# Two heads on one diagonal in the RWKV recurrence of a hybrid decoder step

## The chip, the cores and the metric

The kernel runs on one core of one Trainium2 chip. The metric is the device time of one execution in microseconds (us). A core has a matrix engine (PE, with PEld for its weight loads), three engines for elementwise work (DVE, ACT, POOL) and SP, which here issues every DMA. Each engine takes its instructions in the order in which they were written into its queue before the run.

## The reference

One layer of a decoder trunk on two groups that share the weights: one fresh sequence of 512 tokens, and 8 samples with 8 new tokens each and a past. An RMS norm and an input projection feed two mixers side by side: an RWKV-7 recurrence with 8 heads of 64 channels, and an attention branch with compressed, selected and windowed keys (NSA). Both are gated, merged, projected and added to the residual, and a gated FFN follows. The recurrence is

```
S = S * w_t + (S a_t) b_t^T + v_t k_t^T        per head, S is 64 x 64
y_t = S r_t
```

for the 512 prompt tokens from a zero state, and for each sample's 8 tokens from the state given for it. All is f32.

## The kernel before

The 576 tokens are the free axis; channels lie on the 128 partitions. Weights and activations are split in a high and a low part, and each product of them is three matmuls; all of these are on line 359 (`mm3`). The input projection is 41 column tiles of 16 steps (two column cuts, 8 contraction blocks), and a step is three matmuls. They are generators in a queue called `tiles`, and `pull(n)` writes n steps of them into the program at the place where it is called. So the projection is the filler between the serial steps of the recurrence: `FILL` gives the tiles that are written ahead of the chain of each head pair, `PULL` the steps behind each half step of that chain.

The recurrence works on four pairs of heads, i = 0 to 3. For each pair `rw_operands` builds, for 8 chunks of 64 tokens and one ninth chunk that holds the 64 sample tokens, the operands and the strictly triangular 64 x 64 blocks of pairs of tokens (18 blocks: 9 chunks, 2 heads). The inverse of identity minus block is made in two parts. `rw_inverse` sends the 16 x 16 diagonal blocks through DRAM (`d1`) into 36 partitions of the tile `im`, solves them there on DVE in 15 steps, and sends the results back through DRAM (`d2`) into `dt` (the tile's name in a trace is invt), `b1` (named b), `wt` (in the tile yb) and the diagonal of the blocks. Then `rw_merge_inverse` joins 16 to 32 (lines 661, 668, 671) and 32 to 64 (lines 680, 686) on PE, with copies out of PSUM on ACT and DVE between the rounds. The blocks of both heads lie on partitions 64 to 127 of the state block (`gu`, the same bytes as `gb`), side by side on the free axis, and the 18 blocks go as two groups of nine. `rw_transposed_reads` turns the read operands (line 696) into `at`, which lies in the upper partitions of the tiles im and iw for even pairs, of bk0 and bk1 for odd ones. `rw_fold_inverse` multiplies them by the inverse, a matmul per chunk and head (line 704, 64 rows deep, 64 columns moving); then POOL clears gb's upper half (line 708), since the chain's second matmul reads all 128 rows of it.

`rw_chain` walks the 8 chunks in order (lines 803 and 812 on PE, with DVE between). `rw_samples` does the ninth chunk: it loads the samples' states of one head after the other and transposes them (line 716), reads them (line 733), scales them on POOL, transposes them back (line 743), adds the outer products (line 763) and stores them.

An f32 matmul appears as two MATMUL instructions in the trace, a transpose as one. `PS(tag)` takes the next PSUM bank of a small ring (two banks per pair's parity, tags c0 and c1), and a bank is written again when its reader is done. `slots.t(.., tag)` gives an SBUF slot by its tag. Instructions get their place on each engine from the order in which the code is written, from regions marked high priority (fold, merge and chain steps), and from a scheduler that plans with its own cost figures before the run; semaphores then keep the data right.

## Time and profile before

| what | us |
|---|---|
| median of 3 runs | 1191.52 (1177.23 to 1199.91) |
| the profiled execution's own time | 1183.65 |
| its span, first to last instruction | 1181.8 |
| PE busy in the span | 1128.9 |
| DVE, ACT, POOL busy | 729.4, 523.9, 244.5 |
| mean granted PE clock | 0.971 of full |

The program runs in stages that can be told by the instructions: the norm, the first projections and the operands of pairs 0 and 1 to about 150 us; the joins, chains and samples of the four pairs with projections between them from about 150 to 515; attention to about 650; gate merge, output projection and FFN to the end. The joins of 16 x 16 blocks begin at 154.0, 196.1, 348.5 and 410.3 us. The page gives busy times, which overlap between engines. A matmul's duration holds its whole way through the array, so matmuls that follow each other closely overlap in time; the room that each takes is read from how many follow each other in a stretch. PEclk is the PE clock that was granted, 1.00 being full.

### The profile page before, as it was taken

Reading aid. Unit: us, or ns where it says so; the run is one execution under the profiler, and the core shown is the slowest. Engines: PE = TensorE matmul, PEld = TensorE weight load, DVE = VectorE, ACT = ScalarE, POOL = GpSimd, SP = SyncE. Lnnn points to the kernel's source line nnn. Section 1 sums busy time; section 2 is a strip of 40 time slices with the busy share of each in tenths; the row PEclk is TensorE's granted clock in tenths of the full one; section 3 lists DMA queues with packets and bytes.
Section 4 is the critical chain, followed back from the end, with each engine's and each line's share of the span. In section 5 each row is a group of like instructions: output and inputs, shape, how many; then the busy total and the mean of one; then the engine's idle time right before and its main releaser. Section 6 shows DMA issues by size and latency. Waiting matters only on the chain.

```text
span 1181.8 us, 23148 instructions
## 1 busy us (share of the span) xinstructions
PE 1128.9 (96%) x9117; PEld 1067.7 (90%) x9117; DVE 729.4 (62%) x1461; ACT 523.9 (44%) x1096; POOL 244.5 (21%) x313
## 2 busy tenths in 40 slices
PE   6999899999999999889999999999999999999995
...
GB/s 183 75 59 97 77 88 94 57 59 69 77 145 83 87 133 90 138 31 83 112 104 53 165 152 89 109 37 133 102 70 90 72 142 73 56 89 72 90 72 81
DMA packets 194792, 108.95 MB, mean 92 GB/s; under 512 B 49780, under 2 KB 187970, under 8 KB 194682
## 3 DMA queue, kind: packets, MB, share of 16 engines
...
## 4 chain that ended last, share of the span: by engine, by line
PE 80%; DVE 8%; ACT 4%; DMA 4%; issue 2%; SPq 2%; POOL 0%; POOLq 0%; ACTq 0%; DVEq 0%
PE pd L359 46%; PE pu L359 10%; PE acc L1216 2%; PE ps L704 2%; PE ps L581 2%; SPq L152 1%; PE pT L1201 1%; PE ps L1037 1%; PE pS L1186 1%; DMA wraw<-in_w_in 1%; PE sm L396 1%; DVE invt L155 1%; PE pS L1188 1%; PE pq L733 1%; PE ps L696 1%
## 5 line engine op out<-in xcount | busy, mean ns | idle before, releaser
L359 PE MATMUL pd<-hh,whi 128*128 128x256 f32 (+1 forms) x656 | 203.7, 311 | 8.8 <-ACT pe L407 4.3
L359 PE MATMUL pd<-hh,wlo 128*128 128x256 f32 (+1 forms) x656 | 202.8, 309 | 2.7 <-DVE wlo L155 1.6
L359 PE MATMUL pd<-hl,whi 128*128 128x256 f32 (+1 forms) x656 | 201.5, 307 | 0.0
L359 PE MATMUL pd<-act,hi 128*128 128x288 f32 (+2 forms) x704 | 141.8, 296 | 0.0
L359 PEld LDWEIGHTS pd<-hh,whi 128*128 128x128 f32 x656 | 128.5, 196 | 11.9 <-ACT pe L407 6.3
L359 PEld LDWEIGHTS pd<-hh,wlo 128*128 128x128 f32 x656 | 128.5, 196 | 5.1 <-DVE wlo L155 2.0
L359 PEld LDWEIGHTS pd<-hl,whi 128*128 128x128 f32 x656 | 128.7, 196 | 1.4
L359 PEld LDWEIGHTS pd<-act,hi 128*128 128x128 f32 x704 | 112.6, 188 | 0.1
L155 DVE TENSOR_TENSOR wlo<-wraw,whi 128x1024 fp32r<-128x1024 f32 x60 | 81.0, 1351 | 43.8 <-ACT whi L337 40.0
L359 PE MATMUL pd<-act,lo 128*128 128x288 f32 (+2 forms) x352 | 103.8, 296 | 0.0
L359 PE MATMUL pd<-h2l,hi 128*128 128x288 f32 x352 | 103.6, 295 | 0.0
L359 PE MATMUL pd<-h2h,hi 128*128 128x288 f32 x352 | 103.1, 295 | 0.0
L359 PE MATMUL pd<-h2h,lo 128*128 128x288 f32 x352 | 103.1, 294 | 0.0
L337 ACT CAST hi<-wraw 128x1024 fp32r<-128x1024 f32 (+1 forms) x46 | 46.5, 1012 | 118.8 <-PE pd L359 62.5
L337 ACT CAST whi<-wraw 128x1024 fp32r<-128x1024 f32 x59 | 61.8, 1047 | 83.2 <-PE pd L359 52.7
L155 POOL TENSOR_TENSOR sg<-sg,ut 128x576 f32<-128x576 f32 x11 | 18.1, 1646 | 340.6 <-DVE ut L155 325.5
L155 DVE TENSOR_TENSOR x<-x,pd 128x288 f32<-128x288 f32 (+1 forms) x64 | 28.8, 451 | 65.4 <-PE pd L359 65.4
L155 DVE TENSOR_TENSOR lo<-wraw,hi 128x1024 fp32r<-128x1024 f32 (+1 forms) x46 | 57.0, 1240 | 19.0 <-ACT hi L337 18.8
L359 PEld LDWEIGHTS pd<-h2l,hi 128*128 128x128 f32 x352 | 66.1, 188 | 0.0
L359 PEld LDWEIGHTS pd<-act,lo 128*128 128x128 f32 x352 | 66.0, 188 | 0.0
L359 PEld LDWEIGHTS pd<-h2h,lo 128*128 128x128 f32 x352 | 66.0, 188 | 0.0
L359 PEld LDWEIGHTS pd<-h2h,hi 128*128 128x128 f32 x352 | 65.9, 188 | 0.0
...
## 6 DMA issues: line engine op xcount, KB each, us to landing
...
```

The lines of the kernel that those rows point to most:

```text
L152: (eng or nc.sync).dma_start(out, in_)
L155: return e.tensor_tensor(out, a, b, op)
L337: e[0](hi[:, 0:n], raw[:, 0:n])
L359: i_ = MM(pt[:, 0:w_], lhsT=w, rhs=x[:, c], start=first and k == 0 and j == 0, stop=last and k == n - 1 and j == 2, **kw)
L396: MM(pt[:, 0:HALF], lhsT=l, rhs=r[:, half(a)], start=i == 0, stop=i == len(terms) - 1)
L581: MM(pt[:, c * 128:(c + 1) * 128], lhsT=bk[0:64, c0 + c], rhs=ag[:, c0 + c], start=True, stop=True)
L696: TR(pt[0:64, c * 128:c * 128 + 128], S["ag"][h][:, c0 + c, 0:64], ident)
L704: MM(pw[:, x * 64:x * 64 + 64], lhsT=S["at"][h][:, c], rhs=S["gb"][64:128, c, h], start=True, stop=True)
L733: MM(pq4[0:64, h, :, b], lhsT=s0s[h][0:64, b * 64:b * 64 + 64], rhs=rv[:, :, b], start=True, stop=True)
L1037: MM(po, lhsT=w[:, sl_], rhs=z[:, l, :, hf:hf + 162], start=hf == 0 and l == 0 and j == 0, stop=hf == 1 and l == 7 and j == 2)
L1186: MM(pS[:, 0:nk], lhsT=qs[:, qt * 128:qt * 128 + 128], rhs=kh[:, 0:nk], start=True, stop=False, skip_group_check=True)
L1216: MM(po[:, c0:hf * 256 + 256], lhsT=lv, rhs=ptx[m][:, kk * 256 + q0:kk * 256 + 256], start=name == "slc" and hf == 0 and kt == 0 and j == ...
```

## The change

The two heads of a pair are put on one block diagonal. The pair blocks go to a new tile `nb` (128 rows, nine 128 x 128 squares), head 0 in rows and columns 0 to 63 and head 1 in 64 to 127; the rest of it is cleared once at the start on POOL. `at` becomes a tile of its own, with head 0's reads in rows 0 to 63 and head 1's in rows 64 to 127. Four such tiles are new (nb0, nb1, at0, at1); im and iw shrink from 1152 to 512 columns. The upper half of gb is cleared once at the start and no longer for each pair.

- Join: one group of nine chunks on four 32-row strips at a time, in place of two groups on two strips. The count of matmuls is the same; the copies on ACT go from ten to nine per pair, each group of a round from two PSUM banks to one.
- Fold: one matmul per chunk for both heads, 128 rows deep and 128 columns moving.
- Inverse: the same bytes through d1 and d2, in 8 and 14 DMAs per pair in place of 4 and 7.
- Samples: states of both heads stacked on the rows; 8 transposes in place of 16, 8 reads in place of 16 (with a reads tile `rv` that is zero across heads), one POOL scaling in place of two, 4 transposes back in place of 8, one addition on DVE in place of two. The loads are four DMAs in place of two.
- The keys of the attention branch move to the slots bk0 and bk1, its values to at0 and at1. `FILL` and `PULL` get other numbers, with the same sums.

```
-FILL = (12, 0, 6, 2)
-PULL = (3, 5, 3, 2)
+FILL = (10, 2, 6, 2)
+PULL = (4, 4, 3, 2)
...
+        nbs.extend(wide(x, x).rearrange("p (c x) -> p c x", x=128) for x in ("nb0", "nb1"))
+        ats.extend(wide(x, x).rearrange("p (c x) -> p c x", x=128) for x in ("at0", "at1"))
+        for t_ in nbs:
+            G.memset(t_, 0.0)
+        for t_ in state:
+            G.memset(t_[64:128, 4 * NTOK:8 * NTOK], 0.0)
...
+        S["nb"], S["at"] = nbs[i % 2], ats[i % 2]
...
-        for (rows, x) in ((slice(64, 128), 0), (slice(0, 64), 64)):
-            tt(V, gb[rows], pv_[0:64, :, x:x + 64], bc(mk[0:64, None, x:x + 64], [64, n, 64]), ALU.mult)
+        q = slice(h * 64, h * 64 + 64)
+        tt(V, nb[q, :, q], pv_[0:64, :, 0:64], bc(mk[0:64, None, 0:64], [64, n, 64]), ALU.mult)
+        tt(V, gb[0:64], pv_[0:64, :, 64:128], bc(mk[0:64, None, 64:128], [64, n, 64]), ALU.mult)
         tt(V, ag[64:128], pv_[64:128], bc(mk[64:128, None, :], [64, n, 128]), ALU.mult)
...
+        units = [(slice(h * 9, h * 9 + 9), k, h * 64 + k * 32) for h in range(2) for k in range(2)]
+        for u, k, o in units:
             for b in range(2):
-                o = k * 32 + b * 16
-                dma(d1[k, :, b].rearrange("u s t -> s u t"), gu[64 + o:80 + o, :, o:o + 16])
+                q = slice(o + b * 16, o + b * 16 + 16)
+                dma(d1[k, u, b].rearrange("u s t -> s u t"), nb[q, :, q])
...
+        for u, k, o in units:
+            G.tensor_copy(S["b1"][o:o + 16, :, 0:16], bc(ident[o:o + 16, None, o:o + 16], [16, 9, 16]))
+            dma(S["dt"][o:o + 16], d2[1, k, u, 0].rearrange("u s t -> s u t"))
+        for u, k, o in units:
+            dma(S["b1"][o + 16:o + 32, :, 16:32], d2[0, k, u, 1].rearrange("u s t -> s u t"))
+            if k == 0:
+                dma(S["wt"][o + 16:o + 32, :, 16:32], d2[1, 0, u, 1].rearrange("u s t -> s u t"))
+        for u, k, o in units:
+            q = slice(o + 16, o + 32)
+            dma(nb[q, :, q], d2[0, k, u, 1].rearrange("u s t -> s u t"))
 
     def rw_merge_inverse(S):
 
...
+        nb, dt, b1, wt, ct = (S[x] for x in ("nb", "dt", "b1", "wt", "ct"))
+        quarters, halves = (0, 32, 64, 96), (0, 64)
+        for o in quarters:
+            G.tensor_copy(nb[o:o + 16, :, o:o + 16], bc(ident[o:o + 16, None, o:o + 16], [16, 9, 16]))
+        pz = PS(ct)
+        for u in range(9):
+            for o in quarters:
+                MM(pz[o:o + 32, u * 16:u * 16 + 16], lhsT=nb[o:o + 16, u, o:o + 32], rhs=dt[o:o + 16, u], start=True, stop=True)
+        zt = slots.t(512, f"zt{S['i']}", f"zt{S['par']}")
+        A.copy(zt[:, 0:144], pz[:, 0:144])
+        pw = PS(ct)
+        for u in range(9):
+            z = zt[:, u * 16:u * 16 + 16]
+            for o in quarters:
+                MM(pw[o:o + 16, u * 32:u * 32 + 32], lhsT=z[o:o + 32], rhs=b1[o:o + 32, u], start=True, stop=True)
+            for o in halves:
+                MM(pw[o:o + 32, 288 + u * 16:304 + u * 16], lhsT=b1[o:o + 32, u], rhs=z[o:o + 32], start=True, stop=True)
+        for o in halves:
+            V.tensor_copy(wt[o:o + 32, :, 0:16], pw[o:o + 32, 288:432].rearrange("p (u t) -> p u t", t=16))
+        for o in quarters:
+            A.copy(nb[o:o + 16, :, o:o + 32], pw[o:o + 16, 0:288].rearrange("p (u t) -> p u t", t=32))
+        pz = PS(ct)
+        for u in range(9):
+            for o in halves:
+                MM(pz[o + 32:o + 64, u * 32:u * 32 + 32], lhsT=nb[o:o + 32, u, o + 32:o + 64], rhs=wt[o:o + 32, u],
                    start=True, stop=True)
+        zt = slots.t(512, f"zt{S['i']}", f"zt{S['par']}")
+        for o in halves:
+            A.copy(zt[o + 32:o + 64, 0:288], pz[o + 32:o + 64, 0:288])
+        pw = PS(ct)
+        for u in range(9):
+            for o in halves:
+                q = slice(o + 32, o + 64)
+                MM(pw[o:o + 32, u * 32:u * 32 + 32], lhsT=zt[q, u * 32:u * 32 + 32], rhs=nb[q, u, q], start=True, stop=True)
+        for o in halves:
+            A.copy(nb[o:o + 32, :, o + 32:o + 64], pw[o:o + 32, 0:288].rearrange("p (u t) -> p u t", t=32))
 
     def rw_transposed_reads(S):
-        for h in range(2):
-            for c0 in (0, 4, 8):
-                m = min(4, 9 - c0)
+        for c0 in (0, 4, 8):
+            m = min(4, 9 - c0)
+            for h in range(2):
                 pt = PS(S["ct"])
                 for c in range(m):
                     TR(pt[0:64, c * 128:c * 128 + 128], S["ag"][h][:, c0 + c, 0:64], ident)
-                A.copy(S["at"][h][:, c0:c0 + m], pt[0:64, 0:m * 128].rearrange("p (c x) -> p c x", x=128))
+                A.copy(S["at"][h * 64:h * 64 + 64, c0:c0 + m], pt[0:64, 0:m * 128].rearrange("p (c x) -> p c x", x=128))
 
     def rw_fold_inverse(S):
 
-        for cs in ([(c, 0) for c in range(8)], [(c, 1) for c in range(8)], [(8, h) for h in range(2)]):
+        for c0 in (0, 4, 8):
+            m = min(4, 9 - c0)
             pw = PS(S["ct"])
-            for x, (c, h) in enumerate(cs):
-                MM(pw[:, x * 64:x * 64 + 64], lhsT=S["at"][h][:, c], rhs=S["gb"][64:128, c, h], start=True, stop=True)
-            n, (c, h) = len(cs), cs[0]
-            A.copy(S["ag"][h][:, 0:8, 0:64] if n == 8 else S["agh"][:, 8, :, 0:64],
-                   pw[:, 0:n * 64].rearrange("p (c s) -> p c s", s=64))
-        G.memset(S["gb"][64:128], 0.0)
-
-    def rw_state(S, i, h):
-
-        s0 = slots.t(512, "s0n", f"zt{S['par']}")
-        dma(s0[0:64].rearrange("p (b j) -> p b j", b=8), I["state_rwkv"][0][:, 2 * i + h].rearrange("b i j -> i b j"))
+            for c in range(m):
+                MM(pw[:, c * 128:c * 128 + 128], lhsT=S["at"][:, c0 + c], rhs=S["nb"][:, c0 + c], start=True, stop=True)
+            A.copy(S["agh"][:, c0:c0 + m, :, 0:64],
+                   pw[:, 0:m * 128].rearrange("p (c h x) -> p c h x", h=2, x=64))
+
+    def rw_state(S, i):
+
         pt = PS(S["ct"])
-        for b in range(8):
-            TR(pt[0:64, b * 64:b * 64 + 64], s0[0:64, b * 64:b * 64 + 64], ident[0:64, 0:64])
-        s0t = slots.t(512, "s0t", f"s0{h}")
-        A.copy(s0t[0:64], pt[0:64])
+        for x in range(2):
+            s0 = slots.t(512, "s0n", f"zt{S['par']}")
+            s4 = s0[0:64].rearrange("p (b h j) -> p b h j", b=4, h=2)
+            for h in range(2):
+                dma(s4[:, :, h], I["state_rwkv"][0][4 * x:4 * x + 4, 2 * i + h].rearrange("b i j -> i b j"))
+            for b in range(4):
+                TR(pt[:, (4 * x + b) * 64:(4 * x + b) * 64 + 64], s0[0:64, b * 128:b * 128 + 128], ident[0:64, 0:64])
+        s0t = slots.t(512, "s0t", "s00")
+        A.copy(s0t, pt)
         return s0t
 
...
-        s0s = [rw_state(S, i, h) for h in range(2)]
+        s0t = rw_state(S, i)
+
+        rv = slots.t(512, "rv", "s01")[:, 0:256]
+        G.memset(rv, 0.0)
+        for h in range(2):
+            A.copy(rv[h * 64:h * 64 + 64].rearrange("p (b h x t) -> p h x b t", b=8, h=2, x=2)[:, h],
+                   ag[h][0:64, 8].rearrange("p (x b t) -> p x b t", x=2, b=8))
         pq = PS(ct, "pq")
-        pq4 = pq[:, 0:256].rearrange("p (h x b t) -> p h x b t", h=2, x=2, b=8)
-        for h in range(2):
-            rv = ag[h][0:64, 8].rearrange("p (x b t) -> p x b t", x=2, b=8)
-            for b in range(8):
-                MM(pq4[0:64, h, :, b], lhsT=s0s[h][0:64, b * 64:b * 64 + 64], rhs=rv[:, :, b], start=True, stop=True)
+        for b in range(8):
+            MM(pq[0:64, b * 32:b * 32 + 32], lhsT=s0t[:, b * 64:b * 64 + 64], rhs=rv[:, b * 32:b * 32 + 32], start=True, stop=True)
         sq = slots.t(512, "sq", f"zt{par}")
-        A.copy(sq[0:64, 0:256], pq[0:64, 0:256])
-
-        sos = []
-        for h in range(2):
-            s3 = s0s[h][0:64].rearrange("p (b i) -> p b i", b=8)
-            tt(G, s3, s3, bc(lam[0:64, h, 8:16, None], [64, 8, 64]), ALU.mult)
-            pt = PS(ct)
-            for x in range(4):
-                TR(pt[:, x * 64:x * 64 + 64], s0s[h][0:64, x * 128:x * 128 + 128], ident[0:64, 0:64])
-            so_ = slots.t(512, "so", f"s0{h}")
-            A.copy(so_[:, 0:256], pt[:, 0:256])
-            sos.append(so_)
+        A.copy(sq[0:64, 0:256].rearrange("p (y b t) -> p b y t", y=4, b=8), pq[0:64, 0:256].rearrange("p (b y t) -> p b y t", b=8, y=4))
+
+        s3 = s0t.rearrange("p (b i) -> p b i", b=8)
+        tt(G, s3, s3, bc(S["lams"][:, :, None], [128, 8, 64]), ALU.mult)
+        pt = PS(ct)
+        for x in range(4):
+            TR(pt[:, x * 128:x * 128 + 128], s0t[:, x * 128:x * 128 + 128], ident)
+        so_ = slots.t(512, "so", "s01")
+        A.copy(so_, pt)
...
+        pn = PS(ct)
         for h in range(2):
             ux = slots.t(512, "ux", f"zt{par}")
             tt(V, ux.rearrange("p (b i) -> p b i", b=8), bc(sv[:, 8, h][:, None, :], [128, 8, 64]),
                bc(khb[:, 8:16, None], [128, 8, 64]), ALU.mult)
-            pn = PS(ct)
             for x in range(4):
-                MM(pn[:, x * 64:x * 64 + 64], lhsT=ux[:, x * 128:x * 128 + 128], rhs=bt[:, 8, h], start=True, stop=True)
-            so_ = sos[h]
-            tt(V, so_[:, 0:256], so_[:, 0:256], pn[:, 0:256], ALU.add)
+                MM(pn[:, x * 128 + h * 64:x * 128 + h * 64 + 64], lhsT=ux[:, x * 128:x * 128 + 128], rhs=bt[:, 8, h],
+                   start=True, stop=True)
+        tt(V, so_, so_, pn, ALU.add)
+        o4 = so_.rearrange("p (x h j) -> p h x j", x=4, h=2)
+        for h in range(2):
             for b in range(2):
-                dma(O["s_rwkv"][0].rearrange("(x b) h i j -> b h i x j", b=2)[b, 2 * i + h],
-                    so_[b * 64:b * 64 + 64, 0:256].rearrange("p (x j) -> p x j", x=4))
+                dma(O["s_rwkv"][0].rearrange("(x b) h i j -> b h i x j", b=2)[b, 2 * i + h], o4[b * 64:b * 64 + 64, h])
...
-            t_ = wide(("im", "iw")[bi], "kst", dt=F32R)
+            t_ = wide(f"bk{bi}", "kst", dt=F32R)
...
-            vt = wide(f"bk{bi}", "vtok")
+            vt = wide(f"at{bi}", "vtok")```

Three places in the engines' order follow. In each row stand the source line, the operation and out<-in by the program's names with buffer numbers, and the shape. Lines 672 to 758 of the changed kernel are lines 661 to 743 of the kernel before: 689 and 698 join 32 to 64 (680 and 686 before), 717 folds (704 before).

PE, the second half of pair 0's join, before: 680 and 686 are the two rounds for the two groups of nine, 592 is a product of pair 1's operands, 359 is projection.

```order
L359 MATMUL pd_2042<-hh_98,whi_2038 128x256
L359 MATMUL pd_2042<-hl_99,whi_2038 128x256
L680 MATMUL ps_1562<-yb_941,state_316 32x32 x6
L686 MATMUL ps_1551<-state_316,zt_237_1549 32x32 x9
L680 MATMUL ps_1562<-yb_941,state_316 32x32 x3
L592 MATMUL ps_1332<-state_317,bk_85_320 128x128
L592 MATMUL ps_1332<-state_317,bk_86_321 128x128
L359 MATMUL pd_2042<-hh_98,wlo_2039 128x256
```

The same place now, with 599 and 604 (587 and 592 before) and 708 (696 before) from pair 1.

```order
L359 MATMUL pd_2069<-hl_101,whi_2065 128x256
L689 MATMUL ps_1579<-yb_957,nb_87_322 32x32
L359 MATMUL pd_2069<-hh_100,wlo_2066 128x256
L689 MATMUL ps_1579<-yb_957,nb_87_322 32x32 x17
L599 MATMUL ps_1348<-ident_63,bk_86_321 128x64 x8
L604 MATMUL ps_1358<-state_317,bk_85_320 128x128
L604 MATMUL ps_1358<-state_317,bk_86_321 128x128
L708 MATMUL ps_1463<-ident_63,state_317 64x128 x4
```

Before, the last round of the first group stood among the third round of the second group. Now all eighteen of a round stand together, and other work stands between the rounds.

PE, the fold of pair 0, before: state_316 holds the blocks, im_318 and iw_319 the transposed reads of head 0 and 1.

```order
L704 MATMUL ps_1585<-state_316,im_318 128x64 x3
L704 MATMUL ps_1595<-state_316,iw_319 128x64 x8
L600 MATMUL ps_1342<-ident_63,bk_85_320 128x64
L600 MATMUL ps_1342<-ident_63,bk_86_321 128x64
L696 MATMUL ps_1424<-ident_63,state_317 64x128 x4
L359 MATMUL pd_2070<-hh_98,wlo_2039 128x320
```

The fold of pair 0 now.

```order
L359 MATMUL pd_2132<-hh_92,whi_2128 128x256
L359 MATMUL pd_2132<-hl_93,whi_2128 128x256
L717 MATMUL ps_1622<-nb_87_322,at_89_324 128x128 x4
L717 MATMUL ps_1628<-nb_87_322,at_89_324 128x128 x4
L359 MATMUL pd_2132<-hh_92,wlo_2129 128x256
```

Half as many matmuls, each with 128 moving columns, and they stand in one block in the projection.

SP, the way of pair 0's solved blocks back from DRAM, before: d2p is the DRAM tile, b, invt, yb and state are where the blocks go, nsp and wraw belong to the projections.

```order
L152 DMA d2p_158_897<-iw_319 36x512
L152 DMA d2p_158_897<-im_318 36x512
L152 DMA nsp<-nsp_1969 128x320
L152 DMA b_160_940<-d2p_158_897 16x18x16
L152 DMA invt_906<-d2p_158_897 16x18x16 x2
L152 DMA b_160_940<-d2p_158_897 16x18x16
L152 DMA yb_941<-d2p_158_897 16x18x16
L152 DMA state_316<-d2p_158_897 16x18x16 x2
```

The same place now.

```order
L152 DMA d2p_162_909<-iw_319 36x512
L152 DMA nsp<-nsp_1996 128x320
L152 DMA wraw_2188<-in_w_in 128x8x64
L152 DMA d2p_162_909<-im_318 36x512
L152 DMA b_164_956<-d2p_162_909 16x9x16 x4
L152 DMA invt_922<-d2p_162_909 16x9x16 x4
L152 DMA yb_957<-d2p_162_909 16x9x16 x2
L152 DMA nb_87_322<-d2p_162_909 16x9x16 x4
```

Fourteen DMAs of half the size stand where seven stood, and the last invt load, which the join's first round reads, is now the eighth of them and not the third.

81 lines of the change are left out of this document (19 added, 62 removed).

## The prediction

> **What bounds the kernel now.** I read the page first, then the busy times by stage, then what PE waited for, then the groups of matmuls that the change touches, and the chain of waits where these stand. From the page, the span, PE's busy time and the chain by engine:
>
> ```profile
> span 1181.8 us, 23148 instructions
> PE 1128.9 (96%) x9117; PEld 1067.7 (90%) x9117; DVE 729.4 (62%) x1461; ACT 523.9 (44%) x1096; POOL 244.5 (21%) x313
> PE 80%; DVE 8%; ACT 4%; DMA 4%; issue 2%; SPq 2%; POOL 0%; POOLq 0%; ACTq 0%; DVEq 0%
> ```
>
> PE is busy for 96% of the span and is 80% of the chain, so the end moves with the work on PE, less what its waits take back. The stages, one row each (length, then PE, PEld, DVE, ACT and POOL busy, granted clock, DMA share and rate):
>
> ```profile
> 85.00:180.00 95.00, 89.03 (x853) 83.15 (x853) 54.25 (x115) 41.18 (x80) 24.98 (x39) 0.96 0.34 82
> 180.00:220.00 40.00, 40.00 (x507) 38.38 (x507) 18.08 (x53) 14.47 (x33) 2.15 (x6) 1.00 0.35 93
> 220.00:300.00 80.00, 80.00 (x609) 75.66 (x609) 53.05 (x105) 39.29 (x80) 24.20 (x24) 0.98 0.22 57
> 300.00:345.00 45.00, 42.50 (x321) 39.02 (x320) 32.86 (x73) 22.37 (x43) 14.98 (x20) 0.94 0.39 99
> 345.00:382.00 37.00, 37.00 (x446) 33.69 (x445) 17.13 (x30) 13.35 (x27) 11.16 (x9) 0.82 0.43 124
> 382.00:445.00 63.00, 60.70 (x631) 56.69 (x631) 40.46 (x97) 25.36 (x59) 15.18 (x17) 0.93 0.40 103
> 445.00:520.00 75.00, 70.68 (x521) 62.39 (x522) 47.92 (x130) 39.16 (x115) 29.15 (x45) 0.91 0.35 95
> ```
>
> These 435 us hold all that the change touches. PE stands idle in them for 435 - 419.9 = 15 us only, but its clock is below full, most of all (0.82) in the stretch that holds join and fold of pair 2. The granted clock lost 0.04 x 95 + 0.02 x 80 + 0.06 x 45 + 0.18 x 37 + 0.07 x 63 + 0.09 x 75 = 26 us of clock there. What PE waited for between 85 or 90 and 520 us (us in total, times, longest):
>
> ```profile
> PE pd L359 <- ACT nsp L887: 3.3, 1, 3.3
> PE ps L828 <- DVE so L155: 2.1, 1, 2.1
> PE ps L680 <- ACT gate L1345: 1.7, 1, 1.7
> ```
>
> These are the longest, and only the last is at a join. So the recurrence's serial steps are covered by projections, and a matmul that goes away there shortens the stage by about its own room.
>
> **The change part by part.** The groups on PE from 85 to 520 us that the change touches, and three of other shapes (581, 587, 696) that give prices; the first number behind the bar is the time in which one of the group was on PE, in us:
>
> ```profile
> L581 PE MATMUL ps<-state,bk 64*128 64x128 f32 x128 | 20.2, 297 | 0.0
> L696 PE MATMUL ps<-ident,state 128*64 128x128 f32 x72 | 13.2, 294 | 0.0
> L704 PE MATMUL ps<-state,bk 64*128 64x64 f32 x72 | 10.1, 284 | 0.0
> L671 PE MATMUL ps<-b,zt 32*16 32x32 f32 x288 | 9.9, 189 | 0.0
> L733 PE MATMUL pq<-state,s0t 64*64 64x16 f32 x128 | 9.7, 208 | 0.0
> L661 PE MATMUL ps<-invt,state 16*32 16x16 f32 x288 | 7.7, 179 | 0.0
> L680 PE MATMUL ps<-yb,state 32*32 32x32 f32 x144 | 6.7, 193 | 1.7 <-ACT gate L1345 1.7
> L686 PE MATMUL ps<-state,zt 32*32 32x32 f32 x144 | 6.2, 192 | 0.0
> L704 PE MATMUL ps<-state,iw 64*128 64x64 f32 x36 | 6.2, 330 | 0.0
> L587 PE MATMUL ps<-ident,bk 64*128 64x64 f32 x64 | 6.0, 227 | 0.0
> L716 PE MATMUL ps<-ident,s0n 64*64 64x64 f32 x64 | 6.0, 234 | 0.0
> L704 PE MATMUL ps<-state,im 64*128 64x64 f32 x36 | 5.5, 288 | 0.0
> L743 PE MATMUL ps<-ident,s0t 64*128 64x64 f32 x32 | 3.6, 234 | 0.0
> ```
>
> Fold: 144 instructions of 64 moving columns take 10.1 + 6.2 + 5.5 = 21.8 us, 151 ns each. In their place come 72 of 128 columns. The nearest row with 128 columns moving and 128 weights is 581, 20.2 us for 128, 158 ns: 72 x 158 = 11.4 us, a saving of 10.4. Its depth is 64 rows where the new one has 128; if double columns cost double, the saving is nothing. I take 10.4, since 581 shows what 128 columns cost and 64 columns next to it cost nearly the same.
>
> Reads: 128 take 9.7 us, 76 ns each; 64 remain, with 32 columns moving in place of 16. At 76 ns that is 4.8 us, a saving of 4.8 (nothing, if room went with columns). State transposes: 64 at 6.0 us become 32 with 128 weights and 64 columns, the shape of 587, 6.0 / 64 = 94 ns: 3.0 us saved (at 696's 183 ns, 0.1). Transposes back: 32 at 3.6 become 16 with 128 columns; at 183 ns 2.9 us, 0.7 saved. The matmuls of the outer products stay.
>
> Join: the counts stay. Rounds one and two used two strips already and I leave them as they are; rounds three and four used one strip and get two. The chain of waits gives the room, start, us, what:
>
> ```profile
> 154.75 0.67 PE ps L661 x34
> 177.91 2.26 PE ps L704 x19
> 354.19 0.56 PE ps L661 x35
> 369.56 0.68 PE ps L686 x18
> ```
>
> Round four on one strip takes 0.68 / 18 = 38 ns each, round one on two strips 0.67 / 34 = 20 and 0.56 / 35 = 16. (The fold's 2.26 / 19 = 119 ns says that 151 holds some tail; by it the fold would save 72 x 119 = 8.6.) Rounds three and four together are 288 instructions; by the groups 12.9 us at 45 ns, and at round one's 7.7 / 288 = 27 they would be 7.8: a saving of 5.1, of which I take 5; the lower end is nothing. [...]
>
> Sum of PE's savings: 10.4 + 4.8 + 3.0 + 0.7 + 5 = 24 us, between 0 and about 29.
>
> What the change adds. SP gets 4 + 7 + 2 = 13 more DMAs per pair, 52 in all. Rows of their kind on SP, with the time it takes to issue one (min, median, max in ns), the moment of the last loads before pair 0's join, and two rows of POOL and ACT work that changes:
>
> ```profile
> L152 SPq DMA_DIRECT2D invt<-d2p x8: 303/420/451, 151.0 to 408.5; - x8
> 151.04 0.90 SPq L152 DMA_DIRECT2D invt<-d2p  x2
> L661 PE MATMUL ps<-invt,state x288: 175/178/198, 154.0 to 418.0; 16*32 16x16 f32 x144
> L708 POOL MEMSET state<- x4: 1052/1054/1063, 182.3 to 442.8; 64x1152 f32 x4
> L676 ACT COPY state<-ps 16x288 f32<-16x288 f32 x16 | 6.3, 391 | 6.1 <-DVE yb L673 5.7
> ```
>
> At 0.42 us each the 52 are 22 us of SP. Most of it lies beside a PE that has projections to do. What is queued behind it on SP are the weight loads of the projections (two buffers) and the stores of gates. But on the way into a join little is hidden: pair 0's first round began at 154.0, 2.1 us after SP had issued the last invt load (151.04 + 0.90). The last invt is now the eighth DMA, not the third: 5 x 0.42 = 2.1 us later, and the four extra ones into d1 add up to 4 x 0.42 = 1.7. So 0 to 3.8 us per pair; the new order puts more projection steps ahead of the join, so I take 1 us per pair, 4 in all, ends 0 and 15.
>
> The join is now one series of rounds. Behind its second round ACT does four copies of the 16-row kind in one go, 4 x 0.39 = 1.6 us, which the other group covered half of before. The order has projections, or the next pair's operands, between the rounds; these hide it. I take 2 us in all; if that cover were gone it would be 4 pairs x (1.6 + two copies at 0.39) = 9.5. POOL loses its four memsets of 1.05 us (nobody waited long for them, so nothing), and gets four large ones at the start; the four together would take 2 x 1.05 + 2 x 2 x 1.05 = 6.3 us by that row, in a stretch where POOL is mostly idle: nothing, upper end 2. One addition, one scaling, and two copies fewer on DVE, POOL and ACT, two small copies more on ACT and four on DVE per pair: nothing. New slots for keys and values are free before the attention branch asks for them: nothing. `FILL` and `PULL` move the same 41 tiles; the projections still run out at the end of pair 3's chain: nothing, with 5 either way for stalls that come and go with an order.
>
> Sum: -24 + 4 + 2 = -18 us. Against the profiled execution's 1183.65 (span 1181.8, and 1.85 around it) that is 1165.7. The median of the runs shown is 1191.52, 7.9 above the profiled one; from it 1173.5. I forecast 1173.
>
> **The rivals.** First, the sum is larger because the clock comes back. In the stage rows 26 us of clock are lost; the lowest clock, 0.82, is where small matmuls of the join and 64-row matmuls of the fold stand closest. If shorter and fuller stretches kept half of that, 13 us would come on top: 1160. For: that place. Against: the clock is also low at 445 to 520, where the attention heads begin, and the join's matmuls stay as small. [...] Chance 0.22.
>
> Second, the room is not there: double columns cost double, in fold and reads, so 10.4 + 4.8 goes. Then -18 + 15 = -3: 1189. For: 16 moving columns and 64 differ in the rows. Against: 64 and 128 columns cost 151 and 158 ns. Chance 0.10. The change then does not do what it says.
>
> Third, PE gets shorter but waits for what sets its pace, DVE above all (32.86 of 45 us between 300 and 345). The inverse's 15 steps, the operands and the chain's additions stay, so two thirds of the gain may go into waits: -6, 1186. Against: PE's waits are few in the rows. Chance 0.17.
>
> Fourth, slower: the way into the join decides. If every pair shows all 3.8 us of additional issue and the 2.4 of hand-offs (9.5 / 4), that is 4 x 6.2 = 25, and weight loads behind the 14 DMAs hold PE for another 2 us per pair: -24 + 33 = +9, 1200. It decides from about 6 us per pair on. For: joins start 2 us behind the last load. Against: PE did not wait at any join for a DMA. Chance 0.08.
>
> **How the numbers follow.** The forecast has 0.43. A measurement of this kernel, whose three runs lie 1.9% apart, can tell about 2%, 24 us, from no change. Faster by over 2% (below 1167.7) needs the clock to come back, or the upper end of the forecast's own terms: 0.22 + 0.10 = 0.32. Slower by over 2% (above 1215) needs more than the fourth case: 0.03. The rest is 0.65. The forecast's own range is 1163 to 1183. The range reaches down to the first rival with some of its spread, 1152, and up to the fourth's beginning, 1196.
>
> **What would show it.** In the profile of the changed kernel: the fold at 72 instructions and 11 to 12 us (22 would be the second rival); reads 64 in about 5; rounds three and four together near 8; PE's busy time lower by 20 to 25; the join's first rounds with no wait on a DMA; the clock between 345 and 382 above 0.9 for the first rival. PE waiting at 672, 689 or 698 for a DMA or for ACT copies would show the fourth. If busy time falls and the span doesn't, the third holds. If fold and reads are as cheap as said and no wait grows, but the time is the same, the prediction's reading of PE as the bound is wrong.

## The result

| what | us |
|---|---|
| kernel before, median of all its runs beside it | 1187.72 |
| changed kernel, median of 4 runs | 1142.38 (1140.26 to 1150.21) |
| changed kernel, profiled execution | 1140.26, span 1138.3 |
| mean granted PE clock in the profiled span | 0.988 (before 0.971) |

The changed kernel is faster: 0.9659 of the time before, interval 0.9565 to 0.9752. The forecast was 1173 with a range from 1152 to 1196, so the time lies 31 us below the forecast and 10 below the range. Ratios, and the medians from here on, leave out as slow the runs that took over 1.5% longer than the fastest of their kernel; without its one slow run the kernel before beside this one has a median of 1183.9, so the gain is 41 to 45 us. The same three lines of its page:

```profile
span 1138.3 us, 22837 instructions
PE 1087.3 (96%) x8933; PEld 1030.5 (91%) x8933; DVE 729.0 (64%) x1473; ACT 521.0 (46%) x1092; POOL 242.5 (21%) x329
PE 77%; DVE 9%; ACT 6%; DMA 3%; issue 3%; POOL 1%; SPq 1%; POOLq 0%; ACTq 0%; DVEq 0%
```

The span fell by 43.5 us and PE's busy time by 41.6. PE stood idle for 52.9 us before (1181.8 - 1128.9) and for 51.0 now. So all of the gain is busy time of PE, and it has two parts: matmuls that are gone, and a clock that is higher. Of the span before, 1181.8 x (1 - 0.971) = 34 us were lost to the clock, of the span now 1138.3 x 0.012 = 14. That is 20 of the 43 us.

The busy times by stage, in the same stretches as before (length, then PE, PEld, DVE, ACT and POOL, granted clock, DMA share and rate):

```profile
85.00:180.00 95.00, 88.80 (x875) 82.92 (x874) 56.30 (x129) 44.59 (x87) 23.88 (x45) 0.98 0.37 90
180.00:220.00 40.00, 40.00 (x518) 38.08 (x517) 20.37 (x55) 16.59 (x38) 4.35 (x6) 1.00 0.31 77
220.00:300.00 80.00, 79.56 (x604) 74.52 (x603) 55.74 (x117) 39.92 (x83) 27.34 (x37) 1.00 0.27 70
300.00:345.00 45.00, 41.87 (x409) 39.01 (x410) 36.92 (x72) 21.60 (x39) 15.17 (x14) 0.96 0.45 135
345.00:382.00 37.00, 37.00 (x422) 35.10 (x410) 26.23 (x72) 20.67 (x46) 9.22 (x19) 1.00 0.42 112
382.00:445.00 63.00, 60.52 (x666) 56.12 (x665) 38.28 (x88) 27.83 (x68) 13.06 (x15) 0.97 0.48 124
445.00:520.00 75.00, 66.93 (x473) 54.46 (x474) 59.05 (x166) 51.78 (x154) 33.39 (x55) 0.98 0.32 85
```

The clock is where the difference is most plain: 1.00 in place of 0.82 from 345 to 382, 0.98 in place of 0.91 from 445 on. (The stretches no longer hold the same work in their last third, since the program runs ahead of before.)

The groups of matmuls that the change touches, 85 to 520 us (the first number behind the bar is the time in which one of the group was on PE):

```profile
L717 PE MATMUL ps<-nb,at 128*128 128x128 f32 x72 | 9.7, 277 | 0.0
L672 PE MATMUL ps<-invt,nb 16*32 16x16 f32 x288 | 5.9, 182 | 1.7 <-DMA invt<-d2p 1.6
L681 PE MATMUL ps<-zt,b 32*32 32x16 f32 x144 | 5.1, 178 | 0.0
L679 PE MATMUL ps<-b,zt 32*16 32x32 f32 x288 | 5.0, 191 | 0.0
L750 PE MATMUL pq<-rv,s0t 128*64 128x32 f32 x64 | 4.5, 224 | 0.0
L698 PE MATMUL ps<-nb,zt 32*32 32x32 f32 x144 | 4.2, 193 | 0.0
L689 PE MATMUL ps<-yb,nb 32*32 32x32 f32 x144 | 3.9, 193 | 0.0
L730 PE MATMUL ps<-ident,s0n 64*128 64x64 f32 x32 | 3.9, 236 | 0.9 <-DMA s0n<-in_state_rwkv 0.9
L758 PE MATMUL ps<-ident,s0t 128*128 128x128 f32 x16 | 2.4, 273 | 0.0
```

The fold went from 21.8 to 9.7, reads from 9.7 to 4.5, state transposes from 6.0 to 3.9, transposes back from 3.6 to 2.4, rounds three and four from 12.9 to 8.1, round two from 19.3 (9.9 + 9.4) to 10.1, round one from 7.7 to 5.9. These rows hold the clock too: part of the fold before ran at half clock (pair 2's from 373.5 us to its end at 378.2, at 0.50). The 9.4 is this group of the kernel before:

```profile
L668 PE MATMUL ps<-zt,b 32*32 32x16 f32 x144 | 9.4, 178 | 0.1
```

What PE waited for in 85 to 500 us, the longest one and those at a join or at the samples:

```profile
PE pd L359 <- DVE wlo L155: 4.4, 2, 2.4
PE ps L672 <- DMA invt<-d2p: 1.6, 4, 0.7
PE ps L730 <- DMA s0n<-in_state_rwkv: 0.9, 1, 0.9
```

The waits that the prediction feared are there, but they are small: 1.6 us for the loads of all four joins.

### The profile page after: what moved, and what is told of

The parts are those of the page before. It is cut to its first block, busy times and chain, and to the rows that moved or that the text cites. A ratio compares the mean times of both kernels' runs of the same rounds, so it can differ in the third digit from the quotient of the medians.

```text
span 1138.3 us, 22837 instructions
## 1 busy us (share of the span) xinstructions
PE 1087.3 (96%) x8933; PEld 1030.5 (91%) x8933; DVE 729.0 (64%) x1473; ACT 521.0 (46%) x1092; POOL 242.5 (21%) x329
## 4 chain that ended last, share of the span: by engine, by line
PE 77%; DVE 9%; ACT 6%; DMA 3%; issue 3%; POOL 1%; SPq 1%; POOLq 0%; ACTq 0%; DVEq 0%
PE pd L359 47%; PE pu L359 11%; PE ps L592 1%; PE acc L1231 1%; PE ps L1052 1%; PE pT L1216 1%; PE pS L1201 1%; DVE state L155 1%; DVE wlo L155 1%; PE ps L708 1%; DMA vtok<-in_cache_slc_kv 1%; PE ps L717 1%; DVE state L580 1%; PE pS L1203 1%; ACT P L1210 1%
## 5 line engine op out<-in xcount | busy, mean ns | idle before, releaser
L359 PE MATMUL pd<-hh,whi 128*128 128x256 f32 (+1 forms) x656 | 200.5, 306 | 7.7 <-ACT pe L407 4.9
L359 PE MATMUL pd<-hh,wlo 128*128 128x256 f32 (+1 forms) x656 | 200.2, 305 | 5.4 <-DVE wlo L155 5.3
L359 PE MATMUL pd<-hl,whi 128*128 128x256 f32 (+1 forms) x656 | 198.1, 302 | 0.0
L359 PE MATMUL pd<-act,hi 128*128 128x288 f32 (+2 forms) x704 | 141.8, 296 | 0.0
L359 PEld LDWEIGHTS pd<-hh,whi 128*128 128x128 f32 x656 | 125.4, 191 | 10.6 <-ACT pe L407 6.0
L359 PEld LDWEIGHTS pd<-hh,wlo 128*128 128x128 f32 x656 | 125.4, 191 | 7.7 <-DVE wlo L155 5.9
L359 PEld LDWEIGHTS pd<-hl,whi 128*128 128x128 f32 x656 | 125.4, 191 | 1.2
L359 PEld LDWEIGHTS pd<-act,hi 128*128 128x128 f32 x704 | 112.6, 188 | 0.1
L155 DVE TENSOR_TENSOR wlo<-wraw,whi 128x1024 fp32r<-128x1024 f32 x60 | 78.2, 1304 | 41.0 <-ACT whi L337 40.9
L359 PE MATMUL pd<-act,lo 128*128 128x288 f32 (+2 forms) x352 | 103.8, 296 | 0.0
L359 PE MATMUL pd<-h2l,hi 128*128 128x288 f32 x352 | 103.5, 295 | 0.0
L359 PE MATMUL pd<-h2h,hi 128*128 128x288 f32 x352 | 103.1, 295 | 0.0
L359 PE MATMUL pd<-h2h,lo 128*128 128x288 f32 x352 | 103.1, 294 | 0.0
L155 POOL TENSOR_TENSOR sg<-sg,ut 128x576 f32<-128x576 f32 x11 | 18.1, 1646 | 339.1 <-DVE ut L155 323.9
L155 DVE TENSOR_TENSOR x<-x,pd 128x288 f32<-128x288 f32 (+1 forms) x64 | 28.8, 451 | 65.2 <-PE pd L359 65.2
L155 DVE TENSOR_TENSOR lo<-wraw,hi 128x1024 fp32r<-128x1024 f32 (+1 forms) x46 | 56.7, 1234 | 18.6 <-ACT hi L337 18.6
L359 PEld LDWEIGHTS pd<-h2l,hi 128*128 128x128 f32 x352 | 66.1, 188 | 0.0
L359 PEld LDWEIGHTS pd<-act,lo 128*128 128x128 f32 x352 | 66.0, 188 | 0.0
L359 PEld LDWEIGHTS pd<-h2h,lo 128*128 128x128 f32 x352 | 66.0, 188 | 0.0
L359 PEld LDWEIGHTS pd<-h2h,hi 128*128 128x128 f32 x352 | 65.9, 188 | 0.0
```

The costliest lines, as they stand in the source:

```text
L155: return e.tensor_tensor(out, a, b, op)
L359: i_ = MM(pt[:, 0:w_], lhsT=w, rhs=x[:, c], start=first and k == 0 and j == 0, stop=last and k == n - 1 and j == 2, **kw)
```

## The experiments

Every run lists its span and its mean granted clock, and that gives a second measure. Call span x (1 - clock) the lost clock, and the time less that the net time. The 19 runs of the kernel before that stand beside the experiments took 1175 to 1196 us; their lost clock goes from 24 to 49 us, and their net time only from 1145 to 1152. So within one kernel nearly all of the scatter is clock. The table has medians, for the kernel before over all 19; the clock is given to three digits, so lost clock of one run is good to half a microsecond.

| kernel | time | lost clock | net | ratio to before, interval |
|---|---|---|---|---|
| before | 1187.5 | 38.0 | 1148.4 | 1 |
| before, new `FILL` and `PULL` | 1165.3 | 22.1 | 1143.5 | 0.9855 (0.9797 to 0.9914) |
| changed | 1142.4 | 16.0 | 1126.2 | 0.9659 (0.9565 to 0.9752) |
| changed, old `FILL` and `PULL` | 1161.6 | 30.7 | 1131.1 | 0.9753 (0.9693 to 0.9814) |
| changed, new `FILL` only | 1153.6 | 20.7 | 1132.9 | 0.9695 (0.9619 to 0.9770) |
| changed, new `PULL` only | 1174.6 | 32.8 | 1141.1 | 0.9891 (0.9833 to 0.9950) |
| changed, one tile into chain 2 | 1155.1 | 21.3 | 1133.5 | 0.9718 (0.9659 to 0.9777) |
| changed, join on two strips | 1147.3 | 21.2 | 1126.1 | 0.9650 (0.9591 to 0.9708) |
| changed, fold of 64 rows | 1161.9 | 25.5 | 1137.2 | 0.9760 (0.9701 to 0.9820) |
| changed, that fold on all rows | 1165.5 | 26.2 | 1139.1 | 0.9798 (0.9738 to 0.9859) |
| changed, samples as before | 1162.0 | 23.8 | 1138.7 | 0.9844 (0.9761 to 0.9927) |
| changed, all three undone | 1206.6 | 57.8 | 1147.6 | 1.0185 (1.0099 to 1.0272) |
| changed, twice the small DMAs | 1166.2 | 26.8 | 1140.1 | 0.9871 (0.9810 to 0.9931) |

The kernels stood beside the kernel before on different occasions, when its median was 1190.2, 1180.1 or 1187.7. Nearly all of that is clock: its lost clock was 44.1, 31.8 and 37.9 us, its net time 1147.4, 1148.6 and 1149.4. A difference of times or of lost clock between occasions is therefore good to some 10 us, one of net times to some 3. The first occasion has two strips, both folds and the old numbers in the changed kernel; the second has old samples, all three undone, the doubled DMAs and the kernel before with the new numbers; the third has the probe and the last three. The changed kernel itself was timed on none of these three. The experiments follow in the order in which they were run, the first four together.

### Join on two strips

```
-        for u in range(9):
-            for o in quarters:
-                MM(pz[o:o + 32, u * 16:u * 16 + 16], ...)
+        for u, o in [(u, o) for p in (quarters[:2], quarters[2:]) for u in range(9) for o in p]:
+                MM(pz[o:o + 32, u * 16:u * 16 + 16], ...)
...
```

(and likewise in the other three rounds, where the two heads follow each other)

> Join alone undone: the same matmuls, loads and copies as in the changed kernel, but the two heads one after the other in each round, so that rounds one and two have two strips at a time and rounds three and four one. Theory R (the gain is the room of the matmuls): start to start, rounds two to four took 9.1 + 5.2 + 4.9 us before and 5.0 + 3.4 + 3.5 after, so 7 us come back: about 1149. Theory C (a good part of the gain is the clock, which halves for 3.4 us behind a stretch in which few rows times columns move): the joins of pairs 2 and 3 get longer at few rows, and one to three more stretches at half clock come with it, 1.7 us each: 1151 to 1155. If the strips don't matter: 1142, and the join's gain came from something else (copies, order).

1147.3 us, 0.965 of before (changed kernel 0.966): no difference that can be told. Its groups, with rounds two (678, 680), one (671), four and three (695, 687):

```profile
L678 PE MATMUL ps<-b,zt 32*16 32x32 f32 x288 | 8.8, 189 | 0.0
L680 PE MATMUL ps<-zt,b 32*32 32x16 f32 x144 | 8.7, 177 | 0.0
L671 PE MATMUL ps<-invt,nb 16*32 16x16 f32 x288 | 6.0, 179 | 1.6 <-DMA invt<-d2p 1.6
L695 PE MATMUL ps<-nb,zt 32*32 32x32 f32 x144 | 4.9, 192 | 0.0
L687 PE MATMUL ps<-yb,nb 32*32 32x32 f32 x144 | 4.9, 192 | 0.0
```

The strips do what theory R says of PE's room: round two takes 17.5 us here and 10.1 on four strips, rounds three and four 9.8 and 8.1; round one's row is the same, 6.0 and 5.9. These rows differ by 9 us, but other matmuls share that time: by the pages PE's whole busy time differs by 4.6, 1091.9 here and 1087.3 on four strips, at the same mean clock. And the end does not move: the net time is the same to 0.1 us. PE stands idle for 45.9 us of the 1137.8 here, 5 fewer than in the changed kernel, so by these two profiles the 5 us that four strips save PE waits away again. Which single wait takes it wasn't isolated.

### Fold of 64 rows, and the same fold on all 128

```
-            for c in range(m):
-                MM(pw[:, c * 128:c * 128 + 128], lhsT=S["at"][:, c0 + c], rhs=S["nb"][:, c0 + c], ...)
+        for cs, h in ((range(8), 0), (range(8), 1), ((8,), 0), ((8,), 1)):
+            q, n = slice(h * 64, h * 64 + 64), len(cs)
+            for x, c in enumerate(cs):
+                MM(pw[:, x * 64:x * 64 + 64], lhsT=S["at"][q, c], rhs=S["nb"][q, c, q], ...)
```

and in the second kernel `lhsT=S["at"][:, c], rhs=S["nb"][:, c, q]`.

> Fold alone undone: 144 matmuls of 64 rows and 64 columns, head after head, in place of 72 of 128 by 128 (one ACT copy more). Theory R: the fold's room goes from 7.7 us back to about 144 x 112 ns = 16 us, +8: 1150. Theory C: in the stretches that hold only such matmuls half the rows and half the columns move; behind each of four folds one or two stretches of 3.4 us at half clock, 1.7 us each: +8 and another 3 to 13, 1153 to 1163, with granted clock lost at the folds of pairs 2 and 3 first, where little projection stands between.

> The same 144 matmuls of 64 columns, but 128 rows deep (the other head's rows are zeros and add nothing). Theory R: the same as with 64 rows, 1150, since room goes by the count. Theory C: room as with 64 rows, but twice the rows move, so fewer or none of the half-clock stretches behind folds: 1149 to 1152, and below the kernel with 64 rows by what that one loses in clock. If depth costs room, it is above.

Net times of 1137.2 and 1139.1 against 1126.2: the count of matmuls, with the one ACT copy more per pair that comes with it, is worth 11 to 13 us, whatever their depth. On this R and C agree. The clock behind each fold tells them apart. First the four folds of the kernel with 64 rows, then those with 128, each in a stretch of 17 us that begins about where the fold does (fold's own busy time and count on PE and PEld, then the granted clock):

```profile
173.00:190.00 17.00, 4.25 (x36) 3.84 (x36) 1.00 0.29 73
209.00:226.00 17.00, 5.97 (x36) 5.27 (x36) 0.70 0.10 30
350.00:367.00 17.00, 4.21 (x36) 3.85 (x36) 1.00 0.21 59
424.00:441.00 17.00, 5.06 (x36) 4.50 (x36) 0.60 0.29 84
```

```profile
173.00:190.00 17.00, 4.34 (x36) 4.29 (x36) 1.00 0.39 114
215.00:232.00 17.00, 4.62 (x36) 4.34 (x36) 1.00 0.22 61
365.00:382.00 17.00, 4.45 (x36) 4.28 (x36) 1.00 0.33 85
420.00:437.00 17.00, 4.86 (x36) 4.64 (x35) 0.97 0.39 101
```

Two of four folds of 64 rows lose clock, 0.30 and 0.40 of 17 us, and of the folds on all rows none to speak of. That is theory C at its place. But the sum doesn't follow: the kernel with deep folds loses as much clock in all (26.2 to 25.5), now where PE waited: the clock is 0.50 from 345 to 350 and from 415 to 420 us, and PE was busy for 3.5 and 1.9 of the 5 us ahead of these, with small matmuls of the joins. There waits and small matmuls come together. A variant changes the order of all engines behind the fold, so a lost stretch that goes at one place can come at another.

### Old pulls, and the kernel before with the new ones

> Only the numbers in FILL and PULL as before the change; all matmuls, loads and copies as after. Theory R: the same 41 tiles, so 1142, within 5. Theory C: 1142 as well unless the projection steps no longer stand among the joins and folds of a pair; then up to four stretches of half clock more, 1149. A third theory, that the new order of the projection made the gain (it puts it among the joins and ends stalls), expects 1155 to 1175 here.

> The kernel before with only the new numbers in FILL and PULL. The changed kernel lost 19 us when it got the old numbers. If the new numbers are better by themselves, 1170. If they only fit the shorter joins and folds (more projection in pair 0's chain, less in pair 1's): 1185 to 1200, no gain.

```
-FILL = (10, 2, 6, 2)
-PULL = (4, 4, 3, 2)
+FILL = (12, 0, 6, 2)
+PULL = (3, 5, 3, 2)
```

(the second kernel is the one before with the reverse edit)

This shows where the forecast went wrong. The third theory was right for a good part of the gain, not for all of it: the changed kernel with the old numbers takes 1161.6, and the kernel before gets to 1165.3 by the new numbers alone. In both kernels they bring 4.9 us of net time (1131.1 to 1126.2, and 1148.4 to 1143.5), and 15 to 16 us of clock by the medians of the table (30.7 to 16.0, and 38.0 to 22.1). Beside the kernel before on the same occasion it is 5.1 of net and 9.7 of clock (31.8 to 22.1), so the clock's part is 10 to 16 us. The changed kernel with the old numbers gained 16.3 of net and 13.4 of clock on its own occasion (1147.4 to 1131.1, 44.1 to 30.7): the matmuls moved the clock as well. In the changed kernel part of what the numbers bring is waits: with the old ones PE waits 8.5 us in chain 2 for DVE's state, with the new ones under 1. The stages of the kernel before with the new numbers from 300 us on, where 0.94, 0.82, 0.93 and 0.91 stood:

```profile
300.00:345.00 45.00, 45.00 (x548) 41.91 (x547) 37.27 (x74) 25.22 (x50) 13.07 (x16) 1.00 0.56 157
345.00:382.00 37.00, 37.00 (x310) 35.00 (x309) 24.12 (x59) 14.86 (x31) 15.01 (x18) 1.00 0.31 83
382.00:445.00 63.00, 61.02 (x670) 57.82 (x669) 33.58 (x71) 24.24 (x55) 11.62 (x8) 0.95 0.45 121
445.00:520.00 75.00, 70.00 (x498) 60.06 (x498) 61.08 (x163) 48.97 (x141) 34.27 (x54) 0.93 0.31 82
```

What moved is the place of pair 2's join. Its first round, in the kernel before and then in the same kernel with the new numbers:

```profile
L661 PE MATMUL ps<-invt,state x72: 175/178/198, 348.5 to 354.6; 16*32 16x16 f32 x72
```

```profile
L661 PE MATMUL ps<-invt,state x72: 175/178/198, 324.5 to 330.7; 16*32 16x16 f32 x72
```

With the new numbers it begins 24 us sooner, beside the samples' matmuls of pair 1. Projection stands between its rounds in both kernels, but not beside its fold: in the 10 us that hold the fold PE spends 0.3 us on projection before (369 to 379) and 1.9 with the new numbers (347 to 357), and the clock is 0.72 and 1.00. How that looked in the kernel before, in stretches of 3.4 us around the fold of pair 2 (370.2 to 378.2), all engines:

```profile
366.60:370.10 3.50, 3.50 (x41) 3.25 (x39) 1.20 (x1) 2.25 (x4) 0.00 (x0) 1.00 0.01 3
370.10:373.50 3.40, 3.40 (x39) 3.04 (x35) 1.42 (x4) 1.25 (x3) 0.00 (x0) 1.00 0.46 108
373.50:376.90 3.40, 3.40 (x22) 3.40 (x20) 0.13 (x1) 0.90 (x2) 0.00 (x0) 0.50 0.46 135
376.90:380.30 3.40, 3.40 (x16) 2.83 (x15) 1.53 (x3) 0.84 (x2) 2.90 (x2) 0.50 0.00 0
380.30:383.70 3.40, 3.40 (x16) 3.18 (x16) 0.28 (x1) 0.38 (x1) 0.05 (x1) 0.50 0.00 0
383.70:387.10 3.40, 3.40 (x32) 3.33 (x32) 1.85 (x6) 1.43 (x3) 2.94 (x8) 1.00 0.36 64
```

PE is busy in each of them throughout, and yet the clock is halved behind the first stretch that the fold of 64 rows fills (2.5 of its 3.4 us), and stays so for three. 10.2 us at half clock cost 5.1.

### Samples as before, and all three undone

The first kernel has `rw_state` and `rw_samples` of before in the changed kernel; the second has the join on two strips and the fold of 64 rows as well.

> The samples part alone undone: states, reads and outputs head after head as before the change, everything else as after. Room (R): reads 9.0 against 4.2 us start to start, state transposes 5.3 against 3.2, transposes back 3.0 against 2.0, so about 8 us come back: 1150. Clock (C): before, the clock was halved behind the reads of two pairs (257 and 490 us); with such stretches again 2 to 7 us on top: 1152 to 1157. If the samples lay beside PE's work anyway: 1142.

> The three undone together: join head after head, fold by 64 rows, samples by head. What stays of the change are the tiles, the split loads, the copies and the numbers in FILL and PULL. Measured one by one the three gave 5, 19.5 and (if R holds) 8 us: 1175 if they add up. If the whole gain is in the matmuls and the clock that they cost: 1185 to 1190, the time before the change. If the tiles, the copies and the order carry a part of their own: 1160 to 1172.

Samples: net 1138.7 against 1126.2, 12.5 us, more than the 8 of theory R; lost clock went up by 8. Its reads, state transposes and transposes back:

```profile
L744 PE MATMUL pq<-state,s0t 64*64 64x16 f32 x128 | 9.2, 208 | 0.0
L727 PE MATMUL ps<-ident,s0n 64*64 64x64 f32 x64 | 6.0, 222 | 0.0
L754 PE MATMUL ps<-ident,s0t 64*128 64x64 f32 x32 | 3.5, 231 | 0.0
```

These are 7.9 us more than in the changed kernel (18.7 to 10.8). The other 4 to 5 are not in these groups. By the pages PE stands idle 6.7 us longer (57.7 to 51.0); head by head there are twice as many scalings and additions, and which of these PE waits for wasn't told apart.

All three undone: 1206.6, slower than the kernel before by 1 to 2.7%. Net 1147.6, so the three are worth 21.4 us together (11.0, 12.5 and 0 by themselves). Against the kernel before with the same numbers in `FILL` and `PULL` (net 1143.5) it is 4.1 us dearer, on the same occasion: that is what the tiles, the split loads and the other copies cost, by the medians; the four runs' net times go from 1145 to 1157, so it is a rough figure. The rest of its 41 us against that kernel is clock, 57.8 against 22.1, at two places above all (all engines, clock behind them):

```profile
430.00:470.00 40.00, 39.10 (x429) 35.74 (x428) 3.95 (x9) 9.85 (x24) 2.07 (x2) 0.61 0.30 74
500.00:545.00 45.00, 40.67 (x206) 33.76 (x206) 24.64 (x72) 20.66 (x62) 16.72 (x31) 0.58 0.18 44
```

From 430 to 470 PE is busy for 39 of 40 us at 0.61 of its clock, with join, reads and fold of pair 3 behind one another. From 500 to 545 the last chain steps and the samples of pair 3 stand among attention heads, and PE waits for 4 us as well.

### Twice the small DMAs

```
-                dma(d1[k, u, b].rearrange("u s t -> s u t"), nb[q, :, q])
+                for c in (slice(0, 5), slice(5, 9)):
+                    v = slice(u.start + c.start, u.start + c.stop)
+                    dma(d1[k, v, b].rearrange("u s t -> s u t"), nb[q, c, q])
```

(and so for the loads of solved blocks)

> The 8 + 12 small DMAs of each pair's way through DRAM split once more (22 more DMAs per pair with the stores into d1 and the loads of solved blocks, 88 in all, half the bytes in each). At 0.42 us each on SP the last load that the join's first round reads comes 6 to 7 us later per pair. If that shows at every join, as the prediction's fourth rival has it: +27, 1169. If the projections hide it, as the prediction's own sum has it for most: +4 to +8, 1146 to 1150. Clock theory: stretches at half clock where PE waits at a join, 2 to 7 us on top.

1166.2: net 1140.1, 14 us more, and 11 us more of lost clock. 88 DMAs more cost 24 us, nearly the 27 of the fourth rival's way. But PE waits little for the loads themselves:

```profile
PE ps L680 <- DMA invt<-d2p: 3.2, 4, 1.1
```

3.2 us at four joins, twice what it was. So most of the price isn't at the joins' first round. By the pages PE stands idle 11 us longer (62.1 to 51.0), spread over the program from 180 us to the end; what it waits for there was not told apart. It is a warning for the 52 DMAs that the change added: their price, some 4 us with copies and tiles, isn't the price of the next 52.

### The clock by itself

```
             ff.add_down(c, k0, n_last)
+            if c in PROBE:
+                r, m, n, x = PROBE[c]
+                pp = PS("psf")
+                for _ in range(x):
+                    MM(pp[0:m, 0:n], lhsT=x2[c][0:r, 0:m], rhs=x2[c][0:r, 128:128 + n], start=True, stop=True)
```

> The changed kernel with five blocks of matmuls added in the FFN's last part, where PE is otherwise full and its clock 1.00; their products go nowhere. Each block is some 10 us of one shape: 64 rows deep with 64 columns (the fold before), 128 deep with 64, 128 with 128 (the fold after), 64 with 128, and 32 by 32 on one strip (round four of the join before). Theory C (the clock halves where few rows times columns move): the first and the last block lose clock, the third doesn't; the second and the fourth, half as dense as the third, tell where the bound lies. Theory W (the clock halves only where PE waits): none of them loses clock, since PE waits for nothing inside a block. About 50 us longer than the changed kernel, 55 to 70 with lost clock.

The kernel ran once and took 1210.65 us, 68 more than the changed kernel. The five blocks alone (length, PE busy and instructions, PEld's, granted clock, DMA share and rate): 64 rows with 64 moving columns, 128 with 64, 128 with 128, 64 with 128, all with 128 weight columns, and 32 by 32.

```profile
1087.50:1105.20 17.70, 17.70 (x96) 17.70 (x96) 0.58 0.10 31
1113.90:1124.90 11.00, 10.36 (x94) 10.49 (x94) 1.00 0.17 49
1131.00:1142.20 11.20, 10.21 (x92) 10.34 (x93) 1.00 0.16 48
1149.00:1160.20 11.20, 10.62 (x95) 10.62 (x96) 1.00 0.01 2
1166.50:1180.20 13.70, 12.77 (x300) 12.78 (x300) 0.71 0.01 2
```

Theory C holds and W falls. The blocks of 64 by 64 and of 32 by 32 lose the clock, 0.42 x 17.7 = 7.4 us and 0.29 x 13.7 = 4.0, with PE busy all the time. Around the first of them the stretch of 3.4 us in which the block begins has a clock of 0.89, and each one from 1091 to 1108 has 0.50. The three others, of which two stream half as much as the third, lose none. And at full clock a matmul instruction takes 110 to 112 ns in each of the three (10.36 us / 94, 10.21 / 92, 10.62 / 95), whether it has 64 or 128 rows and 64 or 128 columns.

In the traces of the kernel before and of the changed kernel the clock stands at half in spells of 3.4 us or a multiple. The kernel before has eight of 3.4, three of 6.8 (from 339, 442 and 490 us), one of 10.2 (from 373.5) and one that lasts the final 9.6 us; the changed kernel has five of 3.4 and one over its final 10.2. That a PE which doesn't wait is halved too, if its matmuls are small enough, is what these blocks add (17.7 us at a mean of 0.58, 13.7 at 0.71).

### Half of the numbers, and one tile more

> The changed kernel with FILL new (10, 2, 6, 2) and PULL old (3, 5, 3, 2). With both old it took 1161.6, with both new 1142.4. If FILL carries it (two tiles fewer ahead of chain 0, two more ahead of chain 1): about 1143. If PULL carries it: about 1161. If neither alone does, since chain 0 gets 208 steps and chain 1 112: 1150 to 1170.

> FILL old (12, 0, 6, 2) and PULL new (4, 4, 3, 2): chain 0 gets 256 steps and chain 1 only 64. If PULL carries the gain: about 1143. If FILL does: about 1161. If the placing matters as a whole, 1150 to 1170; PE would then wait in chain 1, which has the fewest projection steps.

> The changed kernel with one of the six tiles ahead of chain 2 moved into it: FILL (10, 2, 5, 2), PULL (4, 4, 4, 2). It lost 1.7 us of clock at each of the joins of pairs 2 and 3 and waited there 0.5 to 1 us. If more projection within a chain covers the next pair's join: 1137 to 1141. If the join of pair 2, which lies ahead of chain 2, misses the tile: 1145 to 1155. It is also a look at how far any small move of the projection goes, whichever way.

| `FILL` | `PULL` | time | net | lost clock |
|---|---|---|---|---|
| (10, 2, 6, 2) | (4, 4, 3, 2) | 1142.4 | 1126.2 | 16.0 |
| (10, 2, 6, 2) | (3, 5, 3, 2) | 1153.6 | 1132.9 | 20.7 |
| (12, 0, 6, 2) | (3, 5, 3, 2) | 1161.6 | 1131.1 | 30.7 |
| (12, 0, 6, 2) | (4, 4, 3, 2) | 1174.6 | 1141.1 | 32.8 |
| (10, 2, 5, 2) | (4, 4, 4, 2) | 1155.1 | 1133.5 | 21.3 |

Neither half carries the whole gain. `PULL` alone makes it worse (chain 1 then has 64 steps and chain 0 256, which may be why). `FILL` alone brings 8 us of the time by the medians, all of it clock (30.7 to 20.7), and nothing of the net time. One tile moved at another place costs 13 us by the medians, 7 of them net. So each of these placings of the same 41 tiles is 11 to 32 us from the best of them, 5 to 15 in net time; since the best was timed on another occasion, the net times are the surer measure. None of the tried sets is better than the one of the change.

## Why the prediction was wrong

**The sum of the matmuls and its costs came out right, in part by luck.** The prediction had -24 for PE's room, +4 for DMAs and +2 for hand-offs, -18. With `FILL` and `PULL` held alike and the clock taken out, the change is worth -17.3 net: 1143.5 to 1126.2 with the new numbers, 1148.4 to 1131.1 with the old. But it got there by errors that cancel: the samples brought 4 more than said, the join 5 less, the costs were 2 lower, and the three parts bring 2 less together than one by one. Its terms:

- Fold: 10.4 forecast, 11.0 net measured. The profile has 72 instructions in 9.7 us where 11 to 12 were said. The shape's price by line 581 was right, and the rival that double columns cost double is dead by the blocks of one shape, 110 to 112 ns for 64 columns and for 128.
- Samples: 4.8 + 3.0 + 0.7 = 8.5 forecast, 12.5 measured. The matmuls gave 7.9 (reads 4.5 us where 4.8 was said, transposes 3.9 and 2.4); the rest belongs to what was put at nothing (one addition, one scaling, fewer copies).
- Join: 5 forecast for rounds three and four, and their group rows agree, 8.1 us where "near 8" was said. But round two, which was left as it was because it used two strips already, gained most, 19.3 to 10.1. And none of it reached the end: on two strips in place of four the net time is the same.
- Costs: 6 forecast, about 4 measured for tiles, loads and copies together. In the profile PE waited 1.6 us for invt in all, not 4.

PE's busy time was to fall by 20 to 25 us. It fell by 41.6 in the profiles, since busy time holds the clock too: 20 us of it are lost clock that came back.

**The step that failed** is the clock, which the sum put at nothing, above all in the step on `FILL` and `PULL`: they "move the same 41 tiles [...] nothing, with 5 either way for stalls that come and go with an order". Their net part, 4.9, lies within those 5. What the step left out is that an order decides which matmuls stand together in a stretch of 3.4 us: the numbers alone gave the kernel before a ratio of 0.9855 beside itself, 15 to 17 us, of which 10 are clock, 10 to 16 by all the runs. The prediction counted the tiles and not what they stood beside. The matmuls' part missed in the same way: with the old numbers the change has a ratio of 0.9753, 29 us where 18 were forecast, 16 net and 13 clock.

**The first rival was the right mechanism with half its size and only part of the cause.** It gave 13 us if the clock came back, and 1160, which is still 18 above the result. By the medians of the table, of 38 us of lost clock 22 went (38.0 to 16.0), and 22 of net time. Its sign, the clock from 345 to 382 above 0.9, came out at 1.00. As to the cause, it named "shorter and fuller stretches" of joins and folds. By the runs the change's own matmuls brought 6 to 13 us of the clock (22.1 to 16.0 with the new numbers, 44.1 to 30.7 with the old beside the kernel before), the numbers 10 to 16; the two can't be parted more closely, since the runs stood on different occasions. The stage rows that were quoted for the rival had the information: 26 us of lost clock, with the lowest rate, 0.82, where small matmuls stood closest. The forecast took none of it back in its likeliest case.

**The second rival**, columns that cost double, fell with the fold's row (72 in 9.7 us) and the probe's blocks (110 to 112 ns for 64 and for 128 columns).

**The third rival**, PE waiting for what sets its pace, shows in one part alone, the join's four strips, and there as 5 us of idle time.

**The fourth**, the way into the join, didn't come. The doubled DMAs show that more of them would not be free, 24 us for 88, but only 3.2 us of that are waits at the joins' first round.

Not settled: which wait takes what the strips save; where the doubled DMAs cost what isn't at the joins; how the clock parts between matmuls and numbers; and which matmuls in a stretch keep the clock, beyond the five shapes tried. Back to back, the block of 64 by 64 lost it (0.58) and that of 64 by 128 didn't (1.00).
